# The RMS norms' sums and broadcasts as pairs of float32r numbers, outside of the latent attention

## The chip, the cores and the metric

The kernel runs on one core of a Trainium2 chip. The core has a matmul engine (TensorE, "PE" in the profile; its weight loads are listed apart as "PEld"), a vector engine (VectorE, "DVE"), a scalar engine (ScalarE, "ACT"), GpSimd ("POOL") and SyncE ("SP", which here issues the weight DMAs). Each engine works through its own queue in the order in which it was written; an instruction that waits for a semaphore holds everything behind it on its engine. The metric is the device time of one execution in microseconds (us); lower is better.

## The reference

A trunk of two layers over 256 tokens of 1024 numbers, all in float32. Each layer is a half-step SwiGLU feed-forward, a mixer (layer 0: multi-head latent attention; layer 1: forgetting attention), a second half-step feed-forward and a gated embedding; every part reads an RMS norm of the residual stream, and a last norm ends the trunk.

```python
def rms_norm(x, g):
    return x * lax.rsqrt(jnp.mean(x * x, axis=-1, keepdims=True) + NORM_EPS) * g

def swiglu(x, w_in, w_out):                      # 1024 -> 2 * 2816 -> 1024
    gate, up = jnp.split(x @ w_in, 2, axis=-1)
    return (jax.nn.silu(gate) * up) @ w_out

for i in range(2):
    h = h + 0.5 * swiglu(rms_norm(h, ffn_norm[i, 0]), ffn_w_in[i, 0], ffn_w_out[i, 0])
    u = rms_norm(h, mix_norm[i])
    h = h + (mla_mixer(u, ...) if i == 0 else fox_mixer(u, ...))
    h = h + 0.5 * swiglu(rms_norm(h, ffn_norm[i, 1]), ffn_w_in[i, 1], ffn_w_out[i, 1])
    h = h + jax.nn.sigmoid(rms_norm(h, ple_norm[i]) @ ple_w_gate[i]) * (p[i] @ ple_w_proj[i])
return rms_norm(h, final_norm)
```

## The kernel before

The residual stream `hT` ("state" in the profile) is held transposed in SBUF: 8 blocks of 128 features, each 128 partitions x 256 tokens. A weight matrix comes in pieces of 128 x 1024 float32 (512 KB) by DMA. Every float32 number that enters a large product is written as two float32r numbers: ACT rounds it ("whi", line 98; "hs", line 213, inside the helper `split`), DVE subtracts that from the original ("wlo", line 102; line 217, the helper `rest`). A product of two such numbers is carried out as three float32r products, two of which share their weights and are one 512-wide product (line 236) with a 256-wide one behind it (line 237); with other shapes they are three products on lines 221 to 223.

`Weights` keeps 4 raw pieces and 7 split pairs. `W.pump()` puts one more piece into the queues: it lets ACT begin the split of up to two pieces ahead, has DVE finish the next one, and then has SP fetch another. The whole program is written in one order by hand (`manual_schedule`), so a `W.pump()` ahead of another line means that its splits stand ahead of that line on ACT and DVE.

A norm's factor per token does not wait for the product: the product is made from the unscaled, gain-weighted stream, and the factor is applied where the result leaves PSUM. Per norm:

- `square`: ACT squares each block ("sq", line 286), POOL adds the squares to "acc" (128 x 256, line 291). What is left is a sum over the 128 partitions.
- `by_token`: PE multiplies "acc", as the stationary operand, with a column of ones, in float32, once for each 128 tokens ("pst", line 305). DVE scales it ("v", line 308), POOL raises it to -1/2 ("rtok", line 310): the factor of a token on that token's partition.
- `by_column`: PE multiplies "rtok", repeated along the free axis, with the identity in float32, again twice ("pb", line 315): the factor of a token along the free axis, the same on all partitions. ACT copies it to SBUF ("rb", line 318).

Where they stand: in a feed-forward (`ffn`), `by_token` follows the third block of products (8 pairs of lines 236 and 237 each), `W.pump()` follows it, and `by_column` stands one block later; the "two" of line 329 then waits for "rb". In the first feed-forward the sums come from ACT (`self.sums`), so only its `by_column` uses PE; there the places are two blocks later. In the embedding gate of layer 0 (`ple`) the products with `p` come first ("pe", evacuated by ACT as "es" on line 817), `by_token` stands after the first half of them, then `W.pump(2)`, and `by_column` ahead of the last of their eight parts. In the last embedding gate (`ple_by_token`) `by_token` stands between the two halves ("fin", line 870); the factor is used by token and there is no `by_column`. In the forgetting attention (`fox`) `by_token` stands in the first group of value products ("pv") and `by_column` in the second.

Of the kernel before, what the change touches and what calls it, by code (L numbers as in the profile page):

```python
# [11 lines left out]
F32 = mybir.dt.float32  # L12
F32R = mybir.dt.float32r
# [6 lines left out]
P = 128  # L20
D = 1024
T = 256
# [119 lines left out]
def trunk(ctx, tc, xT, xt, pT, pos, freq, bf, ffn_first, ffn_in, ffn_out, w_down, w_uq, w_ukv, mla_o,  # L142
# [56 lines left out]
    nc.gpsimd.memset(ones, 1.0)  # L199
    mhalf = const.tile([P, 2], F32, name="mhalf")  # L200
# [61 lines left out]
    class Norm:  # L262
# [37 lines left out]
        def by_token(self):  # L300
            pst = self.sums
            if pst is None:
                pst = psm.tile([P, 2], F32, name="pst", tag="small")
                for t in range(2):
                    nc.tensor.matmul(pst[:, t:t + 1], self.acc[:, t * P:(t + 1) * P], ones[:, :1], start=True,
                                     stop=True)
            v = work.tile([P, 2], F32, name="v")
            nc.vector.tensor_scalar(v, pst, 1.0 / self.dim, EPS, op0=ALU.mult, op1=ALU.add)
            self.rtok = work.tile([P, 2], F32, name="rtok", bufs=3)
            nc.gpsimd.tensor_tensor(self.rtok, v, mhalf, op=ALU.pow)  # L310

        def by_column(self):
            pb = psm.tile([P, T], F32, name="pb", tag="small")
            for t in range(2):
                nc.tensor.matmul(pb[:, t * P:(t + 1) * P], self.rtok[:, t:t + 1].to_broadcast([P, P]), ident,
                                 start=True, stop=True)
            self.rb = work.tile([P, T], F32, name="rb", bufs=3)
            nc.scalar.activation(self.rb, pb, AF.Copy)
            self.rb2 = self.rb.rearrange("p (o t) -> p o t", o=1).to_broadcast([P, 2, T])


    def ffn(norm, nxt, then=None, first=None, meanwhile=None, later=None):
# [39 lines left out]
        for c in range(at, KF):  # L362
            pg = bank("pg")
            block(pg, norm.pair)
            if c == at:
                norm.by_token()
                W.pump()
            else:
                gate(c, pg)
# [187 lines left out]
    def mla(norm, nxt):  # L557
# [4 lines left out]
        norm.by_token()  # L562
# [45 lines left out]
        nkv.by_token()  # L608
# [26 lines left out]
        nq.by_token()  # L635
# [29 lines left out]
    def fox(norm, nxt):  # L665
# [50 lines left out]
        for c in range(4):  # L716
# [3 lines left out]
            for k in range(KD):  # L720
# [4 lines left out]
                if (c, k) == (0, KD - 2):  # L725
                    norm.by_token()
                elif (c, k) == (1, 3):
                    norm.by_column()
                elif (c, k) == (2, 2):
                    steps = gates()  # L730
# [53 lines left out]
    def ple(pp, norm, nxt):  # L784
# [23 lines left out]
        for c in range(2):  # L808
# [12 lines left out]
            W.pump(2 - c)  # L821
        for d in range(KD):
# [113 lines left out]
    for k in range(KD):  # L936
# [6 lines left out]
        if k % 2:  # L943
            W.loaded += 1

# [234 lines left out]
```

## Time and profile before

| | before |
|---|---|
| median of 3 runs | 1001.46 us (1001.19 to 1002.36) |
| the profiled execution's own time | 1001.46 us |
| its span in the trace | 999.7 us |
| PE busy | 988.8 us (99%) |
| DVE, ACT, POOL busy | 740.5, 517.6, 423.7 us |
| DMA | 180.54 MB, mean 181 GB/s |
| granted TensorE clock, mean | 0.998 |

The span runs from the first to the last instruction of the program; the execution's own time has about 2 us around it. A row of the timeline gives start, duration, engine, line, operation, output <- inputs, shapes and how many equal rows are merged; in brackets stands the idle time ahead of it and what ended that. Durations of PE's records overlap, since products are pipelined: what a product holds is read from the distance between starts. A float32r tile is printed as f32 on PE's rows. In a view of waits each row has the total in us, how often, and the longest.

### The profile page before, as it was taken

How to read it: one execution, taken by the hardware profiler on the slowest of the kernel's cores; microseconds unless marked ns; L12 is line 12 of the kernel's file. 1: busy time of each engine (PE TensorE's matmuls, PEld its weight loads, DVE VectorE, ACT ScalarE, POOL GpSimd, SP SyncE). 2: the span in 40 equal slices, each digit the busy share in tenths (PEclk: the TensorE clock that was granted, in tenths of full speed). 3: DMA queues.
4: the chain of work that ended last, by engine and by line, in shares of the span. 5: the costliest groups of instructions: out<-in, count | busy, mean ns of one | idle time of the engine just before them, and what ended most of it. 6: DMA issues, size and time to landing. Idle time of an engine off the chain costs nothing.

```text
span 999.7 us, 16018 instructions
## 1 busy us (share of the span) xinstructions
PE 988.8 (99%) x5940; PEld 875.1 (88%) x5940; DVE 740.5 (74%) x1051; ACT 517.6 (52%) x825; POOL 423.7 (42%) x348
## 2 busy tenths in 40 slices
PE   9999999999999999999999999999999999999996
PEld 7888888998988888889888888899889888888886
DVE  5777879676768787667778876666777778876674
ACT  7555444456655544555555444546445554544552
POOL 0777730110267775111477673211221577671120
PEclk9999999999999999999999999999999999999999
DMA  8566666651456666665366656666443566666561
GB/s 330 177 209 208 190 181 191 187 169 53 132 182 207 189 190 185 193 196 195 127 198 206 192 182 192 180 194 206 151 142 102 189 202 199 189 179 201 178 210 43
DMA packets 51388, 180.54 MB, mean 181 GB/s; under 512 B 5872, under 2 KB 6000, under 8 KB 51312
## 3 DMA queue, kind: packets, MB, share of 16 engines
q1 hardware_dynamic: 50880, 178.75, 57.3%
q8 instruction: 47, 0.77, 0.3%
q10 hardware_dynamic: 432, 0.79, 0.3%
q14 instruction: 29, 0.24, 0.1%
HBM read 178.46 MB, written 1.05 MB: 180 GB/s over the span
## 4 chain that ended last, share of the span: by engine, by line
PE 91%; DVE 4%; ACT 2%; issue 1%; POOL 0%; DMA 0%; POOLq 0%; SPq 0%; ACTq 0%; DVEq 0%
PE pu L236 16%; PE po L236 16%; PE pg L236 16%; PE po L237 8%; PE pu L237 8%; PE pg L237 8%; PE ps L236 4%; PE ps L237 2%; DVE wlo L102 1%; PE ps L221 1%; PE ps L223 1%; PE ps L222 1%; PE pv L221 1%; PE pv L223 1%; PE pv L222 1%
## 5 line engine op out<-in xcount | busy, mean ns | idle before, releaser
L102 DVE TENSOR_TENSOR wlo<-raw,whi 128x1024 fp32r<-128x1024 f32 (+2 forms) x338 | 416.8, 1241 | 17.8 <-ACT whi L98 17.1
L98 ACT ACTIVATE whi<-raw 128x1024 fp32r<-128x1024 f32 (+2 forms) x338 | 336.4, 1027 | 20.9 <-DMA raw<-in_ffn_in_dram 12.9
L331 POOL TENSOR_TENSOR gu<-two 128x256 f32<-128x256 f32 x176 | 235.5, 1339 | 117.9 <-DVE two L329 108.4
L236 PE MATMUL pg<-u,whi 128*128 128x512 f32 x704 | 251.7, 395 | 0.8 <-ACT whi L98 0.4
L236 PE MATMUL pu<-u,whi 128*128 128x512 f32 x704 | 251.1, 395 | 0.0
L236 PE MATMUL po<-hs,whi 128*128 128x512 f32 x704 | 246.0, 394 | 0.0
L237 PE MATMUL pg<-u,wlo 128*128 128x256 f32 x704 | 198.2, 282 | 0.3 <-DVE wlo L102 0.2
L237 PE MATMUL po<-hs,wlo 128*128 128x256 f32 x704 | 198.1, 281 | 0.0
L237 PE MATMUL pu<-u,wlo 128*128 128x256 f32 x704 | 198.0, 281 | 0.0
L236 PEld LDWEIGHTS pg<-u,whi 128*128 128x128 f32 x704 | 132.2, 188 | 32.1 <-DVE u L280 1.3
L236 PEld LDWEIGHTS pu<-u,whi 128*128 128x128 f32 x704 | 132.2, 188 | 30.3
L236 PEld LDWEIGHTS po<-hs,whi 128*128 128x128 f32 x704 | 132.2, 188 | 30.2
L237 PEld LDWEIGHTS pg<-u,wlo 128*128 128x128 f32 x704 | 132.5, 188 | 0.9 <-DVE wlo L102 0.9
L237 PEld LDWEIGHTS pu<-u,wlo 128*128 128x128 f32 x704 | 132.5, 188 | 0.0
L237 PEld LDWEIGHTS po<-hs,wlo 128*128 128x128 f32 x704 | 132.5, 188 | 0.0
L291 POOL TENSOR_TENSOR acc<-acc,sq 128x256 f32<-128x256 f32 x42 | 46.0, 1094 | 173.7 <-ACT sq L286 173.5
L213 ACT ACTIVATE hs<-hid 128x256 fp32r<-128x256 f32 x88 | 36.8, 418 | 142.1 <-POOL hid L349 140.1
L349 POOL TENSOR_TENSOR hid<-sg,gu 128x256 f32<-128x256 f32 x88 | 105.2, 1196 | 7.0 <-POOL gu L331 0.2
L217 DVE TENSOR_TENSOR hs<-hid,hs 128x256 fp32r<-128x256 f32 x88 | 63.5, 721 | 48.6 <-ACT hs L213 48.6
L329 DVE TENSOR_TENSOR two<-pg,rb 128x512 f32<-128x512 f32 x88 | 60.3, 685 | 46.8 <-PE pg L237 38.9
L275 ACT ACTIVATE u<-state 128x256 fp32r<-128x256 f32 x57 | 29.0, 509 | 125.7 <-DVE state L392 104.3
L343 ACT ACTIVATE sg<-gu 128x256 f32<-128x256 f32 x88 | 36.8, 418 | 78.5 <-POOL gu L331 78.5
(247 smaller groups left out, 1189.2 us busy)
## 6 DMA issues: line engine op xcount, KB each, us to landing
raw<-in_ffn_in_dram SPq DMA_DIRECT2D x172, 512.0 KB, 4.1
raw<-in_ffn_out_dram SPq DMA_DIRECT2D x64, 512.0 KB, 3.6
raw<-in_ffn_out_dram SPq DMA_DIRECT2D x32, 384.0 KB, 3.7
raw<-in_fox_qk_dram SPq DMA_DIRECT2D x16, 512.0 KB, 3.5
raw<-in_mla_o_dram SPq DMA_DIRECT2D x8, 512.0 KB, 4.4
raw<-in_ple_gate_dram SPq DMA_DIRECT2D x8, 512.0 KB, 4.6
raw<-in_fox_o_dram SPq DMA_DIRECT2D x8, 512.0 KB, 3.7
raw<-in_ple_rows_dram SPq DMA_DIRECT2D x8, 512.0 KB, 4.7
```

Of the source, the lines that this page charges most:

```text
L98: self.nc.scalar.activation(self.pairs[i][0][:, c], self.raws[i][:, c], AF.Copy)
L102: self.nc.vector.tensor_sub(lo[:, c], self.raws[i][:, c], hi[:, c].bitcast(F32))
L213: nc.scalar.activation(hi, src, AF.Copy)
L217: nc.vector.tensor_sub(lo, src, hi.bitcast(F32))
L236: nc.tensor.matmul(ps, hi, x[:, k], start=k == 0, stop=False)
L237: nc.tensor.matmul(ps[:, 1, :], lo, x[:, k, 0, :], start=False, stop=k == last)
L275: nc.scalar.activation(self.pair[:, b, 0, c], src[:, c], AF.Copy, scale=g)
L291: nc.gpsimd.tensor_add(new, self.acc, sq)
L329: nc.vector.tensor_mul(two, ps, norm.rb2)
L331: nc.gpsimd.tensor_add(gu[c, i], two[:, 0, :], two[:, 1, :])
L343: nc.scalar.activation(sg, gu.pop((c, 0)), AF.Silu)
L349: nc.gpsimd.tensor_mul(hid[c], gu.pop((c, 0)), gu.pop((c, 1)))
```

## The change

Two float32r constants are made at the start: the identity ("identr") and a column pair of ones ("oner"). In `by_token`, ACT rounds "acc" and DVE writes the rest ("accp", by `split`), and PE makes four float32r products of width 2 where it made two float32 products of width 1. A new step `halves` has DVE write the factor as two numbers ("rpair": a rounding copy and the rest), and `by_column` makes four float32r products with "identr" where it made two float32 ones with "ident". `by_token(False)`, used by the three norms of the latent attention, keeps the float32 forms for both. `halves` stands behind the `W.pump` that follows `by_token`, or in the forgetting attention at the second group's first step. So six sums and six broadcasts take the new form. The line numbers grow: 213, 217 become 216, 220; 305 becomes 314 and 315; 308 becomes 320; 315 becomes 339; 318 becomes 342; 817 becomes 844; 870 becomes 899.

```diff
--- before.py
+++ after.py
@@ -197,6 +197,9 @@
     make_identity(nc, ident)
     ones = const.tile([P, P], F32, name="ones")
     nc.gpsimd.memset(ones, 1.0)
+
+    identr = const.tile([P, P], F32R, name="identr")
+    oner = const.tile([P, 2], F32R, name="oner")
     mhalf = const.tile([P, 2], F32, name="mhalf")
     nc.gpsimd.memset(mhalf, -0.5)
@@ -297,23 +300,44 @@
             self.low(b, src)
             self.square(src)
-        def by_token(self):
+        def by_token(self, pairs=True):
             pst = self.sums
             if pst is None:
-                pst = psm.tile([P, 2], F32, name="pst", tag="small")
+                pst = psm.tile([P, 2, 2], F32, name="pst", tag="small")
+                if pairs:
+                    acc = work.tile([P, 2, T], F32R, name="accp", tag="pair2", bufs=4)
+                    split(acc[:, 0, :], acc[:, 1, :], self.acc)
                 for t in range(2):
-                    nc.tensor.matmul(pst[:, t:t + 1], self.acc[:, t * P:(t + 1) * P], ones[:, :1], start=True,
-                                     stop=True)
+                    a = slice(t * P, (t + 1) * P)
+                    if pairs:
+
+                        nc.tensor.matmul(pst[:, t, :], acc[:, 0, a], oner, start=True, stop=False)
+                        nc.tensor.matmul(pst[:, t, :], acc[:, 1, a], oner, start=False, stop=True)
+                    else:
+                        nc.tensor.matmul(pst[:, t, :1], self.acc[:, a], ones[:, :1], start=True, stop=True)
+                pst = pst[:, :, 0]
             v = work.tile([P, 2], F32, name="v")
             nc.vector.tensor_scalar(v, pst, 1.0 / self.dim, EPS, op0=ALU.mult, op1=ALU.add)
             self.rtok = work.tile([P, 2], F32, name="rtok", bufs=3)
             nc.gpsimd.tensor_tensor(self.rtok, v, mhalf, op=ALU.pow)
+            self.rpair = None
+
+        def halves(self):
+
+            self.rpair = work.tile([P, 2, 2], F32R, name="rpair")
+            nc.vector.tensor_copy(self.rpair[:, 0, :], self.rtok)
+            rest(self.rpair[:, 0, :], self.rpair[:, 1, :], self.rtok)
         def by_column(self):
             pb = psm.tile([P, T], F32, name="pb", tag="small")
             for t in range(2):
-                nc.tensor.matmul(pb[:, t * P:(t + 1) * P], self.rtok[:, t:t + 1].to_broadcast([P, P]), ident,
-                                 start=True, stop=True)
+                ps = pb[:, t * P:(t + 1) * P]
+                if self.rpair is None:
+                    nc.tensor.matmul(ps, self.rtok[:, t:t + 1].to_broadcast([P, P]), ident, start=True, stop=True)
+                    continue
+                for i in range(2):
+                    nc.tensor.matmul(ps, self.rpair[:, i, t:t + 1].to_broadcast([P, P]), identr, start=i == 0,
+                                     stop=i == 1)
             self.rb = work.tile([P, T], F32, name="rb", bufs=3)
             nc.scalar.activation(self.rb, pb, AF.Copy)
             self.rb2 = self.rb.rearrange("p (o t) -> p o t", o=1).to_broadcast([P, 2, T])
@@ -365,6 +389,7 @@
             if c == at:
                 norm.by_token()
                 W.pump()
+                norm.halves()
             else:
                 gate(c, pg)
             pu = bank("pu")
@@ -559,7 +584,7 @@
         pq = bank("pq0", (P, T)), bank("pq1", (P, T))
         pkv, pr = bank("pkv", (P, T)), bank("pr", (P, T))
         blocks(pq, norm.pair)
-        norm.by_token()
+        norm.by_token(False)
         table(AF.Exp)
         W.pump()
         block(pkv, norm.pair, norm.by_column, 6)
@@ -605,7 +630,7 @@
         queries(0, 0)
         queries(0, 1)
-        nkv.by_token()
+        nkv.by_token(False)
         W.pump()
         pk = bank("pk", (P, T))
         nc.tensor.matmul(pk, twice, turned, start=True, stop=True)
@@ -632,7 +657,7 @@
             nc.scalar.activation(v[:, t, c * 512:(c + 1) * 512], ps, AF.Copy, scale=nkv.rtok[:, t:t + 1])
         values(0, 0)
-        nq.by_token()
+        nq.by_token(False)
         W.pump()
         values(1, 0)
@@ -724,6 +749,8 @@
                         [u[:, a:a + n] for u in w[k // 4][1:]], k == 0, k == KD - 1)
                 if (c, k) == (0, KD - 2):
                     norm.by_token()
+                elif (c, k) == (1, 0):
+                    norm.halves()
                 elif (c, k) == (1, 3):
                     norm.by_column()
                 elif (c, k) == (2, 2):
@@ -819,6 +846,8 @@
             if c == 0:
                 norm.by_token()
             W.pump(2 - c)
+            if c == 0:
+                norm.halves()
         for d in range(KD):
             ps = bank("ps", (P, T))
             block(ps, norm.pair)
@@ -943,6 +972,9 @@
         if k % 2:
             W.loaded += 1
+    nc.vector.tensor_copy(identr, ident)
+    nc.vector.tensor_copy(oner, ones[:, :2])
+
     def first(ps):
         for k in range(0, KD, 2):
             w, = W.get()
```

How the queues stand at the places where operations are added. In the embedding gate of layer 0, ACT's queue before:

```order
L286 ACTIVATE sq_4938<-state_78 128x256
L98 ACTIVATE whi_4942<-raw_4870 128x1024
L817 ACTIVATE es_4950<-pe_4951 128x512
L817 ACTIVATE es_4950<-pe_4965 128x512
L98 ACTIVATE whi_4986<-raw_4898 128x1024
```

and now ("es" is the copy of the finished "pe" products out of PSUM):

```order
L289 ACTIVATE sq_4957<-state_78 128x256
L98 ACTIVATE whi_4961<-raw_4889 128x1024
L844 ACTIVATE es_4969<-pe_4970 128x512
L844 ACTIVATE es_4969<-pe_4984 128x512
L216 ACTIVATE accp_4999<-acc_4959 128x256
L98 ACTIVATE whi_5010<-raw_4917 128x1024
L98 ACTIVATE whi_5016<-raw_4939 128x1024
```

The new "accp" stands behind both copies and ahead of the next two splits. DVE's queue at the same place, before:

```order
L102 TENSOR_TENSOR wlo_4917<-raw_4849,whi_4916 128x1024
L308 TENSOR_SCALAR v_4982<-pst_4979 128x2
L102 TENSOR_TENSOR wlo_4943<-raw_4870,whi_4942 128x1024
L102 TENSOR_TENSOR wlo_4987<-raw_4898,whi_4986 128x1024
L102 TENSOR_TENSOR wlo_4993<-raw_4920,whi_4992 128x1024
```

and now:

```order
L102 TENSOR_TENSOR wlo_4936<-raw_4868,whi_4935 128x1024
L220 TENSOR_TENSOR accp_4999<-acc_4959,accp_4999 128x256
L320 TENSOR_SCALAR v_5006<-pst_4998 128x2
L102 TENSOR_TENSOR wlo_4962<-raw_4889,whi_4961 128x1024
L102 TENSOR_TENSOR wlo_5011<-raw_4917,whi_5010 128x1024
L328 CAST rpair_5022<-rtok_5008 128x2
L220 TENSOR_TENSOR rpair_5022<-rtok_5008,rpair_5022 128x2
```

The rest of "accp" stands ahead of "v", and the two pieces of "rpair" behind two weight rests.

In the forgetting attention, DVE's queue around the sum, before:

```order
L102 TENSOR_TENSOR wlo_7250<-raw_7182,whi_7249 128x1024
L102 TENSOR_TENSOR wlo_7276<-raw_7203,whi_7275 128x1024
L102 TENSOR_TENSOR wlo_7317<-raw_7231,whi_7316 128x1024
L308 TENSOR_SCALAR v_7349<-pst_7346 128x2
L102 TENSOR_TENSOR wlo_7323<-raw_7253,whi_7322 128x1024
```

and now:

```order
L102 TENSOR_TENSOR wlo_7289<-raw_7221,whi_7288 128x1024
L102 TENSOR_TENSOR wlo_7315<-raw_7242,whi_7314 128x1024
L102 TENSOR_TENSOR wlo_7356<-raw_7270,whi_7355 128x1024
L220 TENSOR_TENSOR accp_7386<-acc_7312,accp_7386 128x256
L320 TENSOR_SCALAR v_7393<-pst_7385 128x2
L102 TENSOR_TENSOR wlo_7362<-raw_7292,whi_7361 128x1024
L328 CAST rpair_7421<-rtok_7395 128x2
L220 TENSOR_TENSOR rpair_7421<-rtok_7395,rpair_7421 128x2
```

The rest of "accp" stands behind the same three weight rests as "v" did, and "rpair" behind one more.

PE's queue there, with what each record waits for, before:

```order
L222 MATMUL pv_7291<-whi,u 128x264
L223 MATMUL pv_7291<-wlo,u 128x264
L305 MATMUL pst<-ones,acc 128x1 [waits Pool_49]
L305 MATMUL pst<-ones,acc 128x1
L221 MATMUL pv_7290<-whi,u 128x264 [waits DVE_49]
```

and now:

```order
L225 MATMUL pv_7330<-whi,u 128x264
L226 MATMUL pv_7330<-wlo,u 128x264
L314 MATMUL pst<-oner,accp 128x2 [waits Activation_49]
L315 MATMUL pst<-oner,accp 128x2 [waits DVE_49]
L314 MATMUL pst<-oner,accp 128x2
L315 MATMUL pst<-oner,accp 128x2
L224 MATMUL pv_7329<-whi,u 128x264
L225 MATMUL pv_7329<-whi,u 128x264
```

The sum waited for POOL's "acc"; now its first record waits for ACT's copy and its second for DVE's rest, in PE's queue ahead of the value products.

## The prediction

> **What bounds the kernel now.** I read the page's busy times and chain first, then what the matmul engine (PE) waits for, then the timeline engine by engine around each place where a norm's sum or broadcast stands.
>
> ```profile
> span 999.7 us, 16018 instructions
> PE 988.8 (99%) x5940; PEld 875.1 (88%) x5940; DVE 740.5 (74%) x1051; ACT 517.6 (52%) x825; POOL 423.7 (42%) x348
> ...
> PE 91%; DVE 4%; ACT 2%; issue 1%; POOL 0%; DMA 0%; POOLq 0%; SPq 0%; ACTq 0%; DVEq 0%
> ```
>
> PE is busy 99% of the span and carries 91% of the chain that ended last. So a change is worth what it does to PE's queue: time that PE's own records take there, and time that PE stands still. The view of PE's waits has, after its rows on the first 10 us:
>
> ```profile
> PE pst L305 <- ACT rb L318: 0.5, 1, 0.5
> ...
> PE pg L236 <- DVE u L280: 0.4, 1, 0.4
> PE po L458 <- ACT ptS L453: 0.3, 1, 0.3
> ...
> PE pt L451 <- DVE pr L444: 0.2, 1, 0.2
> ```
>
> That is 1.4 us in all: PE almost never waits, so there is next to nothing in which a new stall could disappear later. The first of these rows lies in the latent attention, whose norms the change leaves alone.
>
> **What the sums and broadcasts cost on PE now.** The timeline of PE, of its weight loads (PEld) and of the DVE operation that reads the sum, around the sum and the broadcast of one feed-forward norm; the columns are start, duration, engine, line, operation:
>
> ```profile
> 275.72 0.50 PE L305 MATMUL pst<-ones,acc 128*128 128x1 f32 x4
> 276.06 0.19 PEld L236 LDWEIGHTS pu<-u,whi 128*128 128x128 f32 x1
> 276.17 0.19 PEld L237 LDWEIGHTS pu<-u,wlo 128*128 128x128 f32 x1
> 276.26 0.16 DVE L308 TENSOR_SCALAR v<-pst 128x2 f32<-128x2 f32 x1 [1.57 <-PE pst L305]
> 276.40 0.28 PE L237 MATMUL pu<-u,wlo 128*128 128x256 f32 x1
> ...
> 278.61 0.40 PE L236 MATMUL pu<-u,whi 128*128 128x512 f32 x1
> 278.84 0.28 PE L237 MATMUL pu<-u,wlo 128*128 128x256 f32 x1
> 278.96 0.61 PE L315 MATMUL pb<-ident,rtok 128*128 128x128 f32 x4
> 279.63 0.27 PE L237 MATMUL pg<-u,wlo 128*128 128x256 f32 x1
> ```
>
> Two float32 products leave four records: each is carried out as two. A 512-wide float32r product holds PE 0.23 us (278.61 to 278.84). From the sum's first record to the second product behind it are 276.40 - 275.72 = 0.68 us, so the four records take 0.68 - 0.23 = 0.45, or 0.11 each. The broadcast: 279.63 - 278.96 - 0.23 = 0.44, again 0.11 each, though its records are 128 wide and the sum's only 1. What they share is a load of 128 x 128 weights. The float32r load that follows the sum, with nothing but a one-wide record before it, also gives way to the next load after 276.17 - 276.06 = 0.11 us. So both forms are bound by the loads, and a float32r load costs what a float32 load costs.
>
> **The change, part by part.** (1) Six sums (second feed-forward and embedding gate of layer 0; first feed-forward, forgetting attention, second feed-forward and embedding gate of layer 1) and six broadcasts (first feed-forward of layer 0 instead of the last gate) become four float32r products each where there were two float32 ones: four records before, four after, each with one load. I take 4 x 0.11 after as before: 0.0 us on PE. The trace has no float32r product under 256 wide, so I bound it: below, two of four records' worth, 0.22 us less for each of 12 groups, 2.7 us less in all; above, a 128-wide record held as long as the 512-wide one (0.23), 0.12 more for each of 24 broadcast records, 2.9 us more. I take the middle because both quoted groups lie on the load's 0.11.
>
> The Trainium skill, "TensorE: Matmul & The Clock Gate", section on LDWEIGHTS, gives a load as its columns over 1.2 GHz, here an estimate of 107 ns, whatever the data's width; the 0.11 us rows agree, and by it the term is 0.0 too, which speaks against a gain.
>
> (2) Before a sum, ACT now writes a rounded copy of the accumulator and DVE the rest (128 x 256 each), and PE's second record needs that rest. Before a broadcast, DVE writes two 128 x 2 pieces behind the reciprocal root. Nearest rows, the same pair of operations on the same shape in the feed-forwards, and how PE starts again after a wait:
>
> ```profile
> L213 ACT ACTIVATE hs<-hid x88: 417/418/424, 28.7 to 904.7; 128x256 fp32r<-128x256 f32 x88
> L217 DVE TENSOR_TENSOR hs<-hid,hs x88: 424/520/971, 29.2 to 905.2; 128x256 fp32r<-128x256 f32 x88
> ...
> 484.98 0.50 PE L236 MATMUL pg<-u,whi 128*128 128x512 f32 x1 [0.35 <-DVE u L280]
> 485.32 0.27 PE L237 MATMUL pg<-u,wlo 128*128 128x256 f32 x1
> ```
>
> ACT 0.42; DVE 0.42 where POOL is idle beside it (it is, at these places), at the most 0.97. After a wait the first product holds PE 0.34 instead of 0.23: 0.11 more for each stall. Now the places one by one; "second record" is the sum's or broadcast's start plus 0.11.
>
> *First feed-forward, broadcast.*
>
> ```profile
> 22.09 1.06 ACT L98 ACTIVATE whi<-raw 128x1024 fp32r<-128x1024 f32 x1 [1.24 <-DMA raw<-in_ffn_in_dram]
> 23.18 1.22 DVE L102 TENSOR_TENSOR wlo<-raw,whi 128x1024 fp32r<-128x1024 f32 x1 [1.00 <-ACT whi L98]
> 23.75 0.60 PE L315 MATMUL pb<-ident,rtok 128*128 128x128 f32 x4
> ```
>
> A handoff between engines takes 0.03 (ACT's split ends at 23.15, DVE's rest of it starts at 23.18). The two pieces stand on DVE behind that rest, which ends at 24.40; each is priced as "v", also 128 x 2, with a handoff between: 0.16 + 0.03 + 0.16 = 0.35. With a handoff to PE that is 24.78 against 23.86: 0.92 + 0.11 = 1.03 us.
>
> *Embedding gate, layer 0, the sum.*
>
> ```profile
> 454.53 0.85 POOL L291 TENSOR_TENSOR acc<-acc,sq 128x256 f32<-128x256 f32 x1 [4.97 <-ACT sq L286]
> 455.24 1.20 ACT L817 ACTIVATE es<-pe 128x512 f32<-128x512 f32 x2
> 455.65 0.50 PE L305 MATMUL pst<-ones,acc 128*128 128x1 f32 x4
> 456.46 3.48 DVE L102 TENSOR_TENSOR wlo<-raw,whi 128x1024 fp32r<-128x1024 f32 x3
> 456.62 1.61 POOL L310 TENSOR_TENSOR rtok<-v,mhalf 128x2 f32<-128x2 f32 x1 [1.23 <-DVE v L308]
> 458.28 0.71 PE L315 MATMUL pb<-ident,rtok 128*128 128x128 f32 x4
> ```
>
> The accumulator is ready at 455.38, and PE takes it at 455.65. The new copy stands on ACT behind both evacuations "es", which end at 456.44; 0.42 gives 456.86, the handoff 0.03, DVE's rest 0.42 to 457.31, handoff to 457.34. The second record stood at 455.76: 1.58 + 0.11 = 1.69 us.
>
> *The same, broadcast.* In the feed-forward rows "v" starts 276.26 - 275.72 = 0.54 after the sum's first record, 0.43 after its second; here 457.34 + 0.11 + 0.43 = 457.88. Then on DVE: v 0.16, two weight rests (3.48 / 3 each, 2.32), and the two pieces behind them, 0.35. That ends at 460.71, 460.74 on PE. The root on POOL (1.61) is done a microsecond earlier and no longer decides. PE would come at 458.28 + 0.11 + 1.69 = 460.08: 0.66 + 0.11 = 0.77 us.
>
> *Forgetting attention, sum.*
>
> ```profile
> 670.57 4.03 DVE L102 TENSOR_TENSOR wlo<-raw,whi 128x1024 fp32r<-128x1024 f32 x3
> 673.78 0.50 PE L305 MATMUL pst<-ones,acc 128*128 128x1 f32 x4
> ```
>
> The new rest stands on DVE behind three weight rests that run without a break to 674.60: 675.02, on PE 675.05, against 673.89: 1.16 + 0.11 = 1.27 us. Its broadcast comes some 4 us later, behind one weight rest: 0.
>
> *Last embedding gate, sum.*
>
> ```profile
> 964.27 1.11 ACT L870 ACTIVATE fin<-pe 128x512 f32<-128x512 f32 x2
> 964.57 0.50 PE L305 MATMUL pst<-ones,acc 128*128 128x1 f32 x4
> ```
>
> As in layer 0: the evacuations end at 965.38; + 0.42 + 0.03 + 0.42 + 0.03 = 966.28 against 964.68: 1.60 + 0.11 = 1.71 us. The gates behind it read the root long after, and nothing else hangs on it.
>
> *The other three feed-forwards.* The two with the least room, the second of layer 0 (its sum is quoted above, 275.72) and the first of layer 1:
>
> ```profile
> 273.74 1.06 ACT L98 ACTIVATE whi<-raw 128x1024 fp32r<-128x1024 f32 x1 [1.73 <-DMA raw<-in_ffn_in_dram]
> ...
> 488.65 1.04 ACT L98 ACTIVATE whi<-raw 128x1024 fp32r<-128x1024 f32 x1
> 488.85 2.35 DVE L102 TENSOR_TENSOR wlo<-raw,whi 128x1024 fp32r<-128x1024 f32 x2
> 491.66 0.50 PE L305 MATMUL pst<-ones,acc 128*128 128x1 f32 x4
> 492.44 1.62 POOL L310 TENSOR_TENSOR rtok<-v,mhalf 128x2 f32<-128x2 f32 x1 [4.59 <-DVE v L308]
> 494.90 0.61 PE L315 MATMUL pb<-ident,rtok 128*128 128x128 f32 x4
> ```
>
> Layer 0: copy and rest end at 274.80 + 0.42 + 0.03 + 0.42 + 0.03 = 275.70, needed at 275.83. Layer 1: 491.20 + 0.42 + 0.03 = 491.65, needed at 491.77. Both just fit, covered by the three blocks of products between the last residual and the sum; if DVE took 0.97, 0.4 us each. Broadcast: root at 494.06, pieces done 0.41 later at 494.47, needed at 495.01: 0.
>
> (3) At the start DVE casts the identity (128 x 128) and two ones: between 0.16 and 0.42 each, so 0.3 to 0.8 us, ahead of the raw weights' rests. DVE stands idle 1.00 us before 23.18, which covers them: 0. If the later release of a raw buffer delayed the DMA that ACT waits for at 22.09, up to 0.8 us more.
>
> (4) The weights' splits queued behind the new copies come 0.4 us later on ACT and DVE; where PE is stalled by more than that they still come in time: 0.
>
> **Sum.** 1.03 + 1.69 + 0.77 + 1.27 + 1.71 = 6.5 us, and 0.0 for PE's own records. The profiled execution took 1001.46 us (999.7 of span), which is also the median of the runs: 1001.46 + 6.5 = **1007.9 us**, 0.65% slower. A measurement of this kernel can tell about 0.2%, 2.0 us, from no change.
>
> **The rivals.** *A narrow float32r product is slow.* Nothing under 256 wide is in the trace, so a 128-wide record could hold PE 0.23: 1007.9 + 2.9 = 1010.8 us. Against it stands only that the float32 records of that width do not. 13%.
>
> *PE's work in the groups halves.* If the four records took what two take, the sum is 6.5 - 2.7: 1005.2 us. For it: a float32 product is two records now. Against it: four loads remain and each holds 0.11. 9%. The Trainium skill, "FP8 and Floating Point Precision", section "TensorE Precision Notes", has true float32 at four passes through the array; two numbers of one pass each would be half, an estimate that this trace does not bear out, since a float32 product leaves two records here and the loads bind them.
>
> *No slower: the groups become nearly free.* If float32r loads of these groups slipped under their neighbours, 12 x 0.45 = 5.4 us come off and 1002.5 remains, within 0.2%. It decides once a group costs less than 0.08 us, since 12 x 0.37 = 4.5 brings the sum to 2.0. Against it: the float32r load at 276.06 holds its 0.11 with nothing beside it. 5%.
>
> *The stalls don't appear or are given back.* PE would have to lose a later wait for each; there are 1.4 us of such waits, so all of them still leave 1006.5. Only if the splits came ahead of the work now queued before them would there be none: about 1001.5. The order of the changed program says otherwise. 5%, of which 3% faster for reasons I do not see.
>
> **How the numbers follow.** The forecast has 68%, with its own range of 1006.9 to 1009.5 (restarts of zero, 0.55 less in all, and no handoffs, 0.4 less; DVE at 0.97 in two places and a later DMA). The range is 1004.0 to 1011.2: it takes in the halved groups with small stalls and the slow broadcasts. Faster 3%, within 0.2% 7%, slower 90%.
>
> **What would show it.** PE's waits: new rows for pst behind DVE's accp, about 1.6 us at both embedding gates and 1.2 in the forgetting attention, none over 0.3 in the feed-forwards; pb behind DVE's rpair, 0.9 near 24 us and 0.7 near 460 us. The distance from a sum's first record to the second product behind it, in a feed-forward, again 0.68. It is wrong if that distance shrinks to 0.3, if the broadcast's grows beyond 0.9, or if the waits are there and the span is not longer by their sum.

## The result and the profile after

The changed kernel takes 1008.14 us (median of 4 runs, 1007.68 to 1009.66), the kernel before 1001.41 us on the same chip: 6.7 us or 0.65% slower, ratio 1.0065 with a 95% interval of 1.0052 to 1.0078. The forecast was 1007.9 us. The profiled execution is the slowest of the four, 1009.66 us, so its trace has 1.5 us that the median has not; how two executions of this kernel differ is told in experiment 9. Medians here are over all executions, while ratios leave out three that lie far above the rest: one of 1073.7 us of the kernel before beside experiments 1 to 4, one of 1073.7 beside experiment 11, and one of 2525.0 in experiment 5.

The page of the changed kernel: span, busy times (share, instructions), and the engines' shares of the chain that ended last.

```profile
span 1007.7 us, 16037 instructions
PE 993.6 (99%) x5940; PEld 878.2 (87%) x5940; DVE 745.9 (74%) x1071; ACT 519.2 (52%) x831; POOL 424.2 (42%) x348
...
PE 88%; DVE 5%; ACT 3%; issue 2%; DMA 1%; POOL 0%; SPq 0%; POOLq 0%; ACTq 0%; DVEq 0%
```

PE has the same 5940 records. DVE has 20 more instructions and ACT 6 more, and in the chain the two go from 6% together to 8%. PE's waits (total in us, how often, the longest), the rows that are new:

```profile
PE pst L314 <- ACT accp L216: 2.0, 2, 1.0
PE pst L315 <- DVE accp L220: 1.4, 3, 1.1
...
PE pb L339 <- DVE rpair L328: 0.5, 1, 0.5
```

The sums wait 3.4 us in all, a broadcast 0.5. The three stalled sums are at the embedding gates (a wait for ACT's copy and one for DVE's rest at each) and in the forgetting attention (DVE's rest alone). Where they come from, in the timeline of the embedding gate of layer 0, first ACT, then DVE, then PE:

```profile
455.87 1.20 ACT L844 ACTIVATE es<-pe 128x512 f32<-128x512 f32 x2
456.97 0.41 ACT L216 ACTIVATE accp<-acc 128x256 fp32r<-128x256 f32 x1
...
457.41 0.42 DVE L220 TENSOR_TENSOR accp<-acc,accp 128x256 fp32r<-128x256 f32 x1 [0.31 <-ACT accp L216]
...
456.16 0.28 PE L226 MATMUL pe<-q,whi 128*128 128x256 f32 x1
457.43 0.27 PE L314 MATMUL pst<-oner,accp 128*128 128x2 f32 x1 [0.99 <-ACT accp L216]
457.89 0.27 PE L315 MATMUL pst<-oner,accp 128*128 128x2 f32 x1 [0.19 <-DVE accp L220]
```

The copy stands behind both evacuations "es", DVE's rest behind the copy, and PE, whose last product before began at 456.16, starts the sum at 457.43. In the forgetting attention the first record starts at once, and the second waits for DVE's rest, which stood behind three weight rests:

```profile
677.59 0.17 PE L314 MATMUL pst<-oner,accp 128*128 128x2 f32 x1
678.36 0.41 DVE L220 TENSOR_TENSOR accp<-acc,accp 128x256 fp32r<-128x256 f32 x1
678.82 0.27 PE L315 MATMUL pst<-oner,accp 128*128 128x2 f32 x1 [1.06 <-DVE accp L220]
```

What a stall costs is more than the wait in brackets, mostly because the wait counts only from the end of the last record, 0.28 us after its start, where the next one would have started after 0.12.

To see what each place costs I lined up PE's 5940 records of both traces one to one and read by how much the later trace is behind, record by record. That distance grows in steps (from the records just ahead of a place to those just behind it):

| place | step, us | forecast |
|---|---|---|
| first feed-forward, broadcast | 0.80 | 1.03 |
| embedding gate, layer 0, sum | 1.60 | 1.69 |
| behind it, through its broadcast | 1.51 | 0.77 |
| forgetting attention, sum | 1.21 | 1.27 |
| last embedding gate, sum | 1.60 | 1.71 |
| behind it | 1.56 | 0 |
| other feed-forwards, forgetting attention's broadcast | under 0.1 | 0 |
| end of PE | 8.28 | 6.5 |

A start that is 0.19 us earlier and small drifts between the places cancel. The steps of 1.51 and 1.56 are not waits. The sum and the first products behind it at the last gate:

```profile
970.74 0.27 PE L314 MATMUL pst<-oner,accp 128*128 128x2 f32 x1 [0.99 <-ACT accp L216]
971.20 0.27 PE L315 MATMUL pst<-oner,accp 128*128 128x2 f32 x1 [0.19 <-DVE accp L220]
...
971.55 0.58 PE L224 MATMUL pe<-whi,q 128*128 128x512 f32 x1
971.93 0.63 PE L225 MATMUL pe<-whi,q 128*128 128x512 f32 x1
972.36 0.63 PE L226 MATMUL pe<-wlo,q 128*128 128x512 f32 x1
```

The last two 512-wide products stand 0.43 us apart instead of 0.23: the clock is halved. The view by windows has it (length; busy time and records of PE, PEld, DVE, ACT and POOL; granted clock, DMA share, GB/s), first the changed kernel:

```profile
455.00:463.00 8.00, 6.82 (x44) 6.41 (x43) 6.33 (x9) 5.22 (x9) 2.47 (x2) 0.80 0.50 150
...
972.00:975.00 3.00, 3.00 (x9) 2.32 (x8) 2.16 (x2) 0.60 (x1) 1.58 (x1) 0.50 0.93 367
```

and the kernel before:

```profile
453.00:461.00 8.00, 8.00 (x69) 7.91 (x68) 6.83 (x9) 6.47 (x10) 2.46 (x2) 1.00 0.51 170
972.00:975.00 3.00, 3.00 (x15) 2.43 (x14) 1.96 (x3) 2.12 (x2) 0.00 (x0) 1.00 0.32 128
```

Up to PE's end, the trace's record of the granted clock has two stretches at half speed, 459.78 to 463.20 and 971.78 to 975.20 us, 3.41 us each. PE counts as fully busy in the second, with 9 records where there were 15.

What PE's records themselves cost is read in a feed-forward, at the sum and at the broadcast:

```profile
276.31 0.17 PE L314 MATMUL pst<-oner,accp 128*128 128x2 f32 x1
...
276.99 0.28 PE L240 MATMUL pu<-u,wlo 128*128 128x256 f32 x1
...
279.57 0.56 PE L339 MATMUL pb<-identr,rpair 128*128 128x128 f32 x4
279.96 0.45 PE L239 MATMUL pg<-u,whi 128*128 128x512 f32 x1
280.25 0.28 PE L240 MATMUL pg<-u,wlo 128*128 128x256 f32 x1
```

From first record to second product 0.68 at both, against 0.68 and 0.67 before: the float32r group costs what the float32 group cost.

### The profile page after: what moved, and what is told of

It reads as the page before. It is cut to its first block, busy times and chain, and to the rows that moved or that the text cites. A ratio compares the mean times of both kernels' runs of the same rounds, so it can differ in the third digit from the quotient of the medians.

```text
span 1007.7 us, 16037 instructions
## 1 busy us (share of the span) xinstructions
PE 993.6 (99%) x5940; PEld 878.2 (87%) x5940; DVE 745.9 (74%) x1071; ACT 519.2 (52%) x831; POOL 424.2 (42%) x348
## 3 DMA queue, kind: packets, MB, share of 16 engines
HBM read 178.46 MB, written 1.05 MB: 178 GB/s over the span
## 4 chain that ended last, share of the span: by engine, by line
PE 88%; DVE 5%; ACT 3%; issue 2%; DMA 1%; POOL 0%; SPq 0%; POOLq 0%; ACTq 0%; DVEq 0%
PE po L239 16%; PE pu L239 16%; PE pg L239 15%; PE po L240 8%; PE pu L240 8%; PE pg L240 8%; PE ps L239 4%; PE ps L240 2%; DVE wlo L102 2%; PE ps L226 1%; PE ps L225 1%; PE ps L224 1%; DMA slabs<-in_ffn_first_dram 1%; ACT whi L98 1%; DVE u L283 1%
## 6 DMA issues: line engine op xcount, KB each, us to landing
raw<-in_ffn_in_dram SPq DMA_DIRECT2D x172, 512.0 KB, 4.1
raw<-in_ffn_out_dram SPq DMA_DIRECT2D x64, 512.0 KB, 3.7
raw<-in_fox_qk_dram SPq DMA_DIRECT2D x16, 512.0 KB, 3.5
raw<-in_mla_o_dram SPq DMA_DIRECT2D x8, 512.0 KB, 4.3
raw<-in_ple_gate_dram SPq DMA_DIRECT2D x8, 512.0 KB, 5.0
raw<-in_fox_o_dram SPq DMA_DIRECT2D x8, 512.0 KB, 3.6
raw<-in_ple_rows_dram SPq DMA_DIRECT2D x8, 512.0 KB, 4.6
```

## The experiments

My theory: the products cost the same in both forms, and the loss is PE standing still where "accp" and "rpair" queue behind other work, plus half speed where that standstill lowers the clock. The rivals: the new products themselves are dearer or cheaper; or the extra work on ACT and DVE slows the kernel everywhere, stall or not.

**1. Sums alone** ("sums"). `halves` returns at once, so all broadcasts stay float32.

```diff
         def halves(self):
+            return
             self.rpair = work.tile([P, 2, 2], F32R, name="rpair")
```

> All six sums as pairs, all broadcasts float32 as before. Theory: stalls at the sums of both embedding gates and of the forgetting attention, 1.65 + 1.2 + 1.65 = 4.5 us, so 1005.9; and up to 1.5 us more for each of the two gates after which the granted clock falls to one half for one stretch of 3.4 us, as the changed kernel's trace has it: 1005.9 to 1008.9. Rival (the broadcasts' narrow products carry the loss): about 1001.4.

1008.17 us (1006.33 to 1009.82), ratio 1.0060 [1.0045, 1.0076]. PE's waits:

```profile
PE pst L314 <- ACT accp L216: 2.0, 2, 1.0
PE pb L337 <- POOL rtok L322: 1.5, 1, 1.5
PE pst L315 <- DVE accp L220: 1.4, 3, 1.1
```

The sums' waits are those of the full change, 2.0 and 1.4, and so are their steps, 1.61, 1.22 and 1.60. This execution stayed at full clock up to PE's end, yet it took 1008.13 us, since the first norm's factor came late from POOL: 1.5 us of PE waiting (a step of 1.73), at a broadcast that this kernel leaves in float32.

**2. Broadcasts alone** ("bcasts"). The default of `by_token` is turned round, so that all sums stay float32.

```diff
-        def by_token(self, pairs=True):
+        def by_token(self, pairs=False):
```

> All six broadcasts as pairs, all sums float32 as before. Theory: one stall of 0.9 us in the first feed-forward and one of about 0.8 us at the first embedding gate, where the pieces stand behind two weight rests on the vector engine: 1001.4 + 1.7 = 1003.1, the granted clock full throughout. Rival (narrow products slow): 24 x 0.12 = 2.9 us on top, 1006.0. Rival (hidden): 1001.4.

1003.02 us (1002.61 to 1004.39), ratio 1.0014 [1.0004, 1.0023].

```profile
PE pb L339 <- DVE rpair L328: 1.4, 2, 0.8
```

Two waits, and the record-by-record distance grows by 1.13 at the first feed-forward and by 0.76 at the gate of layer 0, where the forecast had 1.03 and 0.77. Sums and broadcasts together, 0.60% and 0.14%, give the 0.65% of the change within the intervals.

**3. Pairs only where nothing stalls** ("fit"). Sums as pairs in the three later feed-forwards, broadcasts in these and in the forgetting attention.

```diff
-        def by_token(self, pairs=True):
+        def by_token(self, pairs=False):
...
-                norm.by_token()
+                norm.by_token(True)
                 W.pump()
-                norm.halves()
+                if not first:
+                    norm.halves()
```

(and no `halves` in the gate of layer 0)

> The new forms only where the trace of the changed kernel shows no stall: sums as pairs in the three later feed-forwards, broadcasts as pairs in these and in the forgetting attention; the rest stays float32. Seven groups of the new form without a stall. Theory (a group of four float32r records holds the matmul engine as long as the float32 one, 0.45 us, and all of the loss is stalls): 1001.4 us, as before, within 0.1%. Rival (two thirds of the passes saved, or half): 7 x 0.22 = 1.5 us faster, 999.9. Rival (narrow float32r records are slow): 4 x 4 x 0.12 = 1.9 us slower, 1003.3.

1001.52 us (1001.33 to 1002.66) against 1002.06, ratio 0.9993 [0.9984, 1.0002]. There is no wait on "accp" or "rpair". Seven of the twelve groups in the new form, with their ACT and DVE work, cost nothing that can be measured: extra work without a stall doesn't slow the kernel, and dearer products (1.9 us more expected) are excluded. Cheaper ones (1.5 us less expected) lie at the edge of the interval, but the record-by-record distance excludes them: from the first feed-forward to PE's end it moves by 0.13 us in all, and upwards. Both rivals fall.

**4. The wait alone** ("wait"). The kernel before, float32 products throughout; at the three stalled places the accumulator goes through one ACT copy and one DVE operation, as the pair does.

```diff
+            if via:
+                a1 = work.tile([P, 2, T], F32, name="via", tag="pair2", bufs=4)
+                nc.scalar.activation(a1[:, 0, :], self.acc, AF.Copy)
+                nc.vector.tensor_tensor(a1[:, 1, :], self.acc, a1[:, 0, :], op=ALU.max)
+                self.acc = a1[:, 1, :]
```

> The kernel before with its float32 products, but at both embedding gates and in the forgetting attention the accumulator goes through one copy on the scalar engine and one operation on the vector engine ahead of the sum, as long as the split. Theory (the queued split, not the number format, makes the stall and with it the clock's fall): as with all sums as pairs, 4.6 us, 1006.0, up to 1.5 us more for each of the two gates with the clock at one half afterwards, so 1006.0 to 1009.0. Rival (the float32r records themselves): 1001.4.

1006.89 us (1005.73 to 1009.15), ratio 1.0051 [1.0034, 1.0068].

```profile
PE pst L310 <- DVE via L305: 4.0, 3, 1.5
PE pb L320 <- POOL rtok L315: 1.6, 1, 1.6
```

Without one float32r product of the new kind, most of the loss is there. The steps are 1.72, 1.33 and 1.71 us (a float32 sum starts only on the complete operand, while the pair's first record starts on the copy). This execution, 1009.15 us, also has one half-speed stretch behind the first gate, a step of 1.39, and the late first norm, 1.9.

**5. All twelve pairs, none late** ("early"). The split of the accumulator stands ahead of the work it queued behind: ahead of the evacuations at both gates, with the sum in the second half of the products; ahead of `W.pump()` in the forgetting attention; in the first feed-forward `halves` ahead of `W.pump()`; at the gate of layer 0 the broadcast inside the first gate's block. An excerpt:

```diff
                 norm.by_token()
+                if first:
+                    norm.halves()
                 W.pump()
-                norm.halves()
+                if not first:
+                    norm.halves()
...
+                if (c, i) == (0, 1):
+                    norm.early()
+                elif (c, i) == (1, 1):
+                    norm.by_token()
```

> All twelve pairs of the change, but none late: in the first feed-forward the two pieces stand ahead of the weight rest; at the embedding gates the accumulator's split stands ahead of the evacuations and the sum half a group of products later, and the first gate's broadcast moves into the first gate block; in the forgetting attention the split stands ahead of the weight split of step 3. Theory (all of the loss is the place in the scalar and vector engines' queues): no stall over 0.3 us at the sums and broadcasts, 1001.4 to 1002.0. Rival (the pairs cost on the matmul engine): 1003 to 1007.

1001.57 us (median of 11) against 1001.49, ratio 1.0000 [0.9991, 1.0009]. No wait on "accp" is left, and of the pairs' waits only this one, in an execution of 1002.66 us whose first norm was late:

```profile
PE pb L344 <- DVE rpair L333: 1.1, 1, 1.1
```

So the whole loss is a matter of place in the queues: the same computation in another order costs nothing that can be measured (the interval allows 0.9 us either way).

**6. and 7. The price of a group** ("rep32r", "rep32"). The broadcast's products nine times over at four places, on "fit" in float32r and on the kernel before in float32; the result is that of the last repeat. The edit in float32r; the other kernel repeats `[0, 1]` nine times at the same four places:

```diff
-            for t in range(2):
+            for t in [0, 1] * (1 if self.rpair is None else 9):
```

> The kernel with pairs only where they fit, the broadcast's four float32r products made nine times over at the three later feed-forwards and in the forgetting attention (the same result): 4 places x 32 more 128-wide records. Theory (a record holds the matmul engine for its weight load, 0.11 us): 128 x 0.112 = 14.3 us more, 1015.8. Rival (half): 1008.6. Rival (narrow products slow, 0.23): 1031.

> The kernel before, with the broadcast's two float32 products (four records) made nine times over at the same four places. Theory: the same 14.3 us, 1015.8, so that both forms of the group cost the same. Rival (a float32 group costs more than a pair's): more than the float32r repeats by 1 us or more.

1015.48 us, ratio 1.0136 [1.012, 1.0151], and 1016.36 us, ratio 1.0145 [1.0131, 1.0158]. In the timelines, first float32r, then float32:

```profile
278.91 4.13 PE L339 MATMUL pb<-identr,rpair 128*128 128x128 f32 x36
282.87 0.45 PE L239 MATMUL pg<-u,whi 128*128 128x512 f32 x1
```

```profile
280.18 4.18 PE L315 MATMUL pb<-ident,rtok 128*128 128x128 f32 x36
284.12 0.47 PE L236 MATMUL pg<-u,whi 128*128 128x512 f32 x1
```

3.96 and 3.94 us for 36 records, 0.11 each in both forms. "A narrow float32r product is slow", "the work halves" and "the groups become nearly free" are all excluded.

**8. The standstill filled** ("filled"). The changed kernel with ten 256-wide bf16 products of zeros, written to a PSUM bank that nobody reads, ahead of the sum at both gates (the zeros, "warm", are made earlier in the program for it).

```diff
+            if fill:
+                idle = bank("idle", (P, T))
+                for _ in range(fill):
+                    nc.tensor.matmul(idle, warm[:, :P], warm, start=True, stop=True)
```

> The changed kernel, with ten 256-wide bf16 products of zeros (about 1.1 us, their result is not used) in the matmul engine's queue directly ahead of the sum at both embedding gates, where it stands still anyway. Theory (the stall lets the granted clock fall to one half for the next stretch of the clock's 3.4 us grid): the stalls stay as long, the clock stays at 1.0 behind both gates, and 1.5 us behind the last gate and 0.7 behind the first are saved: about 1007.5 where the changed kernel's profiled execution had 1009.7, and no slot of 0.43 us for a 512-wide product behind the last gate. Rival (the slow stretch comes from narrow float32r products or from the weights' supply): the stretch stays, 1009.7 in such an execution.

1007.48 us (1007.4 to 1009.95), ratio 1.0062 [1.0048, 1.0076]. The products behind the last gate's sum in the execution of 1007.49 us:

```profile
971.05 0.48 PE L227 MATMUL pe<-whi,q 128*128 128x512 f32 x1
971.36 0.39 PE L228 MATMUL pe<-whi,q 128*128 128x512 f32 x1
971.60 0.40 PE L229 MATMUL pe<-wlo,q 128*128 128x512 f32 x1
971.83 0.39 PE L227 MATMUL pe<-whi,q 128*128 128x512 f32 x1
```

They are 0.23 apart again: no half speed behind either gate, with the stalls of the sums unchanged (steps 1.60, 1.22 and 1.60). And the broadcast's wait at the gate of layer 0, missing from the changed kernel's trace, is there:

```profile
PE pb L346 <- DVE rpair L335: 0.4, 1, 0.4
```

Its step is 0.56. The steps of this execution add up to 0.45 + 1.60 + 0.56 + 1.22 + 1.60 = 5.4 us, the forecast's list without half speed. That it was the filling that kept the clock up is not shown: other executions kept it at a gate without any filling, as the next experiment and the last part of the explanation below have it. The slowest of the four took 1009.95 us and was not traced.

**9. The changed kernel once more** ("after_again"), for its clock.

> The changed kernel once more, one look, for its clock. If the half-speed stretches behind the two embedding gates depend on where a fixed raster of 3.41 us cuts the standstill, their number differs from execution to execution of the same program (none, one or two of them), each with 1.5 us more in PE's offset, and the waits on pst stay at about 1.6, 1.2 and 1.6 us. If they belong to the program, both gates show them again.

1008.46 us. The waits on "pst" are again 2.0 and 1.4, and the steps 1.61, 1.21 and 1.60. The clock, in the same windows as above:

```profile
455.00:463.00 8.00, 6.82 (x44) 6.53 (x43) 6.67 (x10) 5.34 (x9) 2.48 (x2) 0.79 0.49 151
972.00:975.00 3.00, 3.00 (x16) 2.45 (x16) 2.43 (x3) 0.65 (x2) 1.61 (x1) 1.00 0.94 352
```

One half-speed stretch instead of two (a step of 1.39 behind the first gate), and 1.2 us less, although its start was 0.7 us later. The sums' waits belong to the program; the number of half-speed stretches belongs to the execution.

**10. One product pair for sum and broadcast** ("col"). On "fit": in the three later feed-forwards 128 columns of ones are the stationary operand and the pair moves, 256 wide, so that every partition gets every token's sum and no broadcast is needed. The root is then taken of 128 x 256 numbers.

```diff
+            for i in range(2):
+                nc.tensor.matmul(pst, onesr, acc[:, i, :], start=i == 0, stop=i == 1)
+            v = self.rb = work.tile([P, T], F32, name="rb", bufs=3)
+            nc.vector.tensor_scalar(v, pst, 1.0 / self.dim, EPS, op0=ALU.mult, op1=ALU.add)
+            nc.gpsimd.tensor_tensor(self.rb, v, mhalf[:, :1].to_broadcast([P, T]), op=ALU.pow)
```

> The pairs only where they caused no stall (as in 'fit'), and in the three later feed-forwards one step more: one pair of 256-wide float32r products with 128 columns of ones as the stationary operand gives the sum of each token on all 128 partitions at once, so that the separate sum and broadcast (two groups of 0.45 us on PE) become two products of 0.11 to 0.12 us each. The root is then taken by POOL on 128x256 numbers instead of 128x2. Theory (PE's own records are the whole cost where nothing waits): three times 0.90 - 0.23 = 0.67, 2.0 us less than before: 999.4 us, ratio 0.998, and PE's waits as before. Rival: POOL's root on 128x256 is not ready when the gate is read, some block later; each microsecond by which it is late then costs at most one on PE in three places, above 1001.5 us if it is late by 0.7 us each.

1112.62 us, ratio 1.1096 [1.1081, 1.1112]: the rival, far beyond the price I gave it.

```profile
L340 POOL TENSOR_TENSOR rb<-rb,mhalf 128x256 f32<-128x256 f32 x3 | 126.2, 42050 | 16.0 <-DVE rb L339 16.0
```

POOL's root takes 42 us (third number from the "|", mean ns), 0.16 us per number of a partition. On 128 x 2 it had taken at most 1.6.

**11. The same with the root on ACT and DVE** ("colsqrt").

```diff
-            nc.gpsimd.tensor_tensor(self.rb, v, mhalf[:, :1].to_broadcast([P, T]), op=ALU.pow)
+            nc.scalar.activation(v, v, AF.Sqrt)
...
+        def inverse(self):
+            nc.vector.reciprocal(self.rb, self.rb)
...
                     norm.column()
                 W.pump()
+                if not first:
+                    norm.inverse()
```

> As 'col', but the root of 128x256 numbers leaves POOL, where one took 42 us: ACT takes the square root (0.42 us, with one more table load of 1.28 us ahead of it) right after DVE's 'v', and DVE the reciprocal after the weight rest. Theory: PE's own records are the whole cost where nothing waits, three times 0.67 less: 999.4 us, ratio 0.998, with no new row in PE's waits. Rival: the factor comes too late for the gate or the weights' splits behind the table load come too late; before, the first use of the factor started 4.3 us behind the sum's first record, and the new path takes about 0.5 + 0.3 + 1.3 + 0.4 + the reciprocal (not in the trace, 0.5 to 2 us) = 3 to 4.5 us, so up to 0.5 us in three places, 999.4 to 1001 us.

999.43 us (998.94 to 1000.82) against 1001.49, ratio 0.9977 [0.9967, 0.9986]. It is the one version faster than both kernels. One of the three places, PE and then the root's way over DVE, ACT and DVE:

```profile
277.37 0.40 PE L337 MATMUL pst<-accp,onesr 128*128 128x256 f32 x2
277.61 0.39 PE L240 MATMUL pu<-u,whi 128*128 128x512 f32 x1
...
277.80 0.42 DVE L339 TENSOR_SCALAR rb<-pst 128x256 f32<-128x256 f32 x1 [1.02 <-PE pst L337]
...
278.26 0.42 ACT L340 ACTIVATE rb<-rb 128x256 f32<-128x256 f32 x1 [0.64 <-DVE rb L339]
...
279.28 1.74 DVE L343 RECIPROCAL rb<-rb 128x256 f32<-128x256 f32 x1
```

The two products take 0.24 us of PE (277.37 to 277.61) where sum and broadcast took 0.90, three times over: 2.0 us, the measured gain. The reciprocal takes 1.74 us and ends 3.65 us behind the sum's start; PE's waits have no row for it.

## Why the prediction was right, and where it was not

The time and its sign were right, and for the reason given: PE's own records are unchanged (0.68 to 0.68; 0.11 per record in both forms in experiments 6 and 7), and the loss starts with the queues' stalls. Point by point:

- *The sums' stalls*, forecast 1.69, 1.27 and 1.71: measured 1.60, 1.21 and 1.60. Adding up the work queued ahead of each new operation gave each within 0.11 us.
- *First feed-forward's broadcast*, 1.03: measured 0.80 in the profiled execution, 0.47, 0.45 and 1.13 in "after_again", "filled" and "bcasts". The start of the program is not the same in each execution, and the slack here differs with it.
- *Broadcast at the gate of layer 0*, 0.77: not a wait in the changed kernel's trace, but a step of 0.76 in "bcasts" and 0.56 in "filled". In the changed kernel PE ran at half speed ahead of it and came late itself, at 461.07, when the first piece of "rpair" was written (460.93) and the second nearly (461.12). The wait was covered by a loss of 1.51 that the forecast did not have.
- *The later feed-forwards and the forgetting attention's broadcast*, 0: right, though by little slack (0.12 us in the forecast's working).
- *The start's casts*, 0: nothing above the start's own scatter is seen. Ahead of the first broadcast, the traces lie between 0.6 us before and 0.6 us behind the kernel before, and the earliest, "wait", is one without the casts.
- *Missing*: half speed behind the gates, 1.4 to 1.6 us for each stretch. The step that failed is the rule "0.11 more for each stall", read from a restart after a stall of 0.35 us. The delay of a sum's second record was 1.58, 1.20 and 1.58 us, close to the forecast's 1.58, 1.16 and 1.60; the restart behind it then cost 0.02 us instead of 0.11 at full clock, but at both gates of the profiled execution another 1.5, because the clock halved.

So the agreement of 1008.14 with 1007.9 is luck in part. The stalls alone come to 0.80 + 1.60 + 1.21 + 1.60 = 5.2 us, which would be 1006.7; with two half-speed stretches PE's end is 8.28 us later, 1009.7 (1009.66 in the first profile). The median lies between: the missing half speed, about 1.5 us a stretch, and the stalls that were forecast too long or were covered, 1.3 us together, partly cancel. What the three executions that were not traced lost by half speed is not shown; their mean granted clocks, 0.996 to 0.998, are too coarse to count stretches, and a late first norm, as in "sums", leads to the same time. Half speed was not on the forecast's list of risks.

*What lowers the clock.* The two stretches of the first profile begin 512.0 us apart, 150 times 3.413, and each lasts 3.41: they lie on a fixed raster. The Trainium skill, "TensorE: Matmul & The Clock Gate", Part 1, describes a free-running activity window of 3413 ns, and the trace agrees to the digit. The same page of the Trainium skill, "Why this matters for your kernels", asks for no PE-idle gaps over about 3 us and has the clock fall after one idle window; here the clock fell after far shorter gaps, and the measurement decides. Each trace also has half speed behind PE's end, which lies on the same raster (in the first profile from 1002.50, nine windows behind 971.78), so the windows of the other traces can be placed too. Counting in each raster window how long PE had no record, and how many columns the records that start in it stream (512 for a 512-wide product, 2 for a record of a pair's sum):

| trace, place | idle in the window, us | columns | next window |
|---|---|---|---|
| changed kernel, gate of layer 0 | 1.18 | 3336 | half |
| changed kernel, last gate | 1.18 | 3080 | half |
| changed kernel, forgetting attention | 0.47, then 0.59 | 5810, 5174 | full |
| again, gate of layer 0 | 1.18 | 2824 | half |
| again, last gate | 1.12 | 4098 | full |
| again, forgetting attention | 1.05 | 4150 | full |
| "sums", gate of layer 0 | 0.51, then 0.67 | 5888, 4616 | full |
| "sums", last gate | 0.76, then 0.42 | 5120, 5128 | full |
| "wait", gate of layer 0 | 1.45 | 2564 | half |
| "wait", last gate | 1.23 | 4096 | full |
| "colsqrt", first feed-forward | 1.39 | 3456 | full |
| "wait", first feed-forward | 1.63 | 2816 | full |

Half speed followed four of the six windows that hold all or most of a gate's standstill, and did not follow where the raster cut it in two, as in "sums". Idle time alone doesn't decide, as 1.23, 1.39 and 1.63 show. The columns streamed fit better: at most 3336 ahead of half speed and at least 3456 ahead of full speed, but for the last row. What the chip counts stays open. So does the effect of the filling in experiment 8: there a window ended at 457.23, within the filled stretch, so that the first gate's standstill was cut in two anyway, and at the last gate "after_again" kept the clock unfilled.

## What to carry to other kernels

Where one engine is busy 99% of the time, price an edit by what it puts between a producer and that engine's next instruction, and add up what is already queued ahead of it on each helper engine: here that gave every sum's stall within 0.11 us, while the products' form was worth nothing. Then ask whether the operand could be started earlier in those queues, which here brought the whole loss back. A saving comes from fewer products on the busy engine, as in the last experiment, not from products of another type that load as many weights.

## What the runs showed of the hardware

- A float32 product of 128 x 128 weights leaves two records of 0.11 us, with 1 column or with 128; two float32r products with 2 or 128 columns cost the same. The weight load, which all of them share, fits as the bound; no run changed the load alone.
- A standstill of about 1.2 us can cost another 1.4 to 1.6 us, since the clock may halve for one raster window of 3.41 us behind it, and whether it does varies from execution to execution.
- POOL's power took 42 us on 128 x 256, where 128 x 2 took 1.6 at most. DVE's reciprocal takes 1.74 us there, ACT's square root 0.42 after a table load of 1.28.
- In some executions PE waits up to 1.6 us for the first norm's factor from POOL, also in "wait", "sums" and "colsqrt", whose broadcast there is that of the kernel before. In "wait" POOL's power started 1.0 us later and took 1.58 us instead of 0.71; why is not shown.
